# Seven block products for the last wide layer: the second product in three sweeps, with its weight sums made earlier by GpSimd

## The chip, the core and the metric

The kernel runs on one core of a Trainium2 chip. The core has five engines that run their own instruction streams: TensorE (PE in the profile; PEld is its weight load), VectorE (DVE), ScalarE (ACT), GpSimd (POOL) and SyncE (SP, which here only issues DMAs). The metric is device time in microseconds, the median of three runs; lower is better.

## What is computed

A two-layer encoder over 512 tokens of width 1024. Layer 0 has a grouped-query attention and a latent attention side by side, layer 1 a neighbourhood attention with 16 heads. Behind each attention stands a squared-ReLU MLP of width 4096, and at the end an RMS norm. The change touches the MLP of layer 1, and what runs beside the second attention:

```python
def sq_relu_mlp(h, w_up, w_down):
    u = jax.nn.relu(h @ w_up)
    return (u * u) @ w_down
...
        h = h + sq_relu_mlp(rmsnorm(h, norm_ffn[layer]), ffn_w_up[layer], ffn_w_down[layer])
    return rmsnorm(h, final_norm)
```

Everything is float32.

## The kernel before

**Precision.** TensorE works on rounded numbers (fp32r). Each operand is kept as a high part and a low part (`whi`, `wlo` for weights: ACT rounds, DVE subtracts), and a product is three matmuls: high by high, high by low, low by high. The residual stream is kept transposed in SBUF (`hT`, features on the partitions, 8 tiles of 128x512).

**Memory.** 30 slots of 128x1024 float32 are handed out and given back by hand, first in, first out (`Slot`, L65). Raw weights go into a free slot while more than `reserve[0]` are free, otherwise into one of four `raw` buffers. PSUM's eight banks carry four names: mm (3), s (2), t (2), o (1); `group` (L406) hands out four at a time, in turns (`flip`).

**The order of the work.** `plan` (L233) lists the weight groups in the order of their use; `weights(i)` (L237) issues loads five groups ahead of group i and makes high and low parts two groups ahead. A scheduler orders each engine's instructions by when they become ready, except inside `fixed_order` (L957): there TensorE, ACT, DVE and GpSimd run in the order in which the code is written. The second attention runs so. SP's queue is always ordered by the scheduler; every engine takes its own queue strictly in order.

**Plain and seven-product matrix products.** `product` (L415) is the plain one, 512 columns of tokens to a matmul. `Seven` (L314) computes a product of two by two blocks with seven block products instead of eight: the weight blocks are first combined into seven (`seven_chunk`, L295: three GpSimd sums L302 to L304, then ACT L308 and DVE L309), the tokens too (`sums`, `split`), and `Seven.run` (L376) issues 21 matmuls of 256 columns for each pair of tiles (L388 to L390) and combines the seven results when they leave PSUM (L396 to L400).

**The MLP of layer 1** (`mlp`, L1250, called at L1670 with the tail `last`). The 4096 hidden features are 32 tiles of 128. `first_product` (L1110) makes them: six by plain products, the other 26 by thirteen calls of `Seven.run`, two tiles each. `SIZES[1]` = (6, 8, 6, 8, 4) cuts them into stages:

- six tiles (plain), then their part of the second product (plain, 48 groups of three matmuls);
- eight tiles (four calls of `Seven.run`), then their part (plain, 64 groups, L501 to L503);
- six, eight and four tiles (nine calls); the plain part of the six (48 groups), and beside it the DVE makes and splits the token sums of the eight (`convert`, L1243);
- the eight tiles in seven products, four calls of `Seven.run`; beside the last two, `turn(j, 0)` (L1614) transposes the first half of `hT` back to tokens;
- the last four tiles (`down`, L1621), with tokens on the output partitions, mixed with `turn(j, 1)`, the final norm and the stores.

**The second attention** (`attend_C`, L1412). 16 heads, two halves each. In each half TensorE makes the scores of two units, DVE adds the bias (L1441, loaded from DRAM by SP, L1504), ACT takes the exponential (L1460), DVE the reciprocal (L1429), and GpSimd scales (`norm`, L1430). TensorE transposes the result in the next head (`turn`, L1446) and multiplies by the values (`finish`, L1465). `rest` (L1482) calls `norm` twice, and fills TensorE's time in between with work of `fill`: the next projections and the output projection. GpSimd also issues copies of keys and queries (L1338, L1358, L1359); SP issues L1334 and L1363, which follow those.

Of the kernel before, what the change touches and what calls it, by code (L numbers as in the profile page):

```python
# [35 lines left out]
def encoder_kernel(ctx: ExitStack, tc: tile.TileContext, ins, out, dbg=None):  # L36
# [242 lines left out]
    def catch_up():  # L279
        take_up(off_d)  # L280
        take_up(off_a)
# [491 lines left out]
    rope_q(0)  # L773


    kst = Slot()

    def ev_kr(b):
# [331 lines left out]
    def first_product(l):  # L1110
# [7 lines left out]
        xp = [s_.pair() for s_ in X]  # L1118
        U, R = [], []
        rb = keep([P, S], F32, "rb")  # L1120
        state = dict(c=SIZES[l][0], ids=None, plain=False, split=iter(()))
        x7 = Seven(KD)

        def ev(j, b):
# [62 lines left out]
        def ahead():  # L1187
            state["ids"] = x7.plan(w, P * state["c"])

        def stage(n, raw=0, more=0):  # L1190

            if not state["plain"]:
                plain()
            left = n + raw + more - len(U)
            while left:
                i = state["ids"]
                state["c"] += 2
                left -= 2
                if left:
                    ahead()  # L1200
                for _ in x7.run(i, raw_evac if more <= left < more + raw else pair_evac):
# [13 lines left out]
    def bias_rows():  # L1215
        R, Fi, Fe = Slot(F32), Slot(F32), Slot(F32)
        rpb = ins["od_rpb"][0]
        for qr in range(8):
            SP.dma_start(R.t[16 * qr : 16 * qr + 16, 0:248],
                           rpb.rearrange("h a b -> h (a b)")[:, (7 - qr) * 31 : (7 - qr) * 31 + 248])  # L1220
            yield
        POOL.memset(Fi.t[:, 0:376], NEG)
        POOL.memset(Fe.t[:, 256:512], NEG)
        rv = R.t[:, 0:248].rearrange("p (k d) -> p d k", d=31)
        POOL.tensor_copy(Fi.t[:, 0:376].rearrange("p (j k) -> p j k", k=8)[:, 15:31, :], rv[:, 7:23, :])
        POOL.tensor_copy(Fe.t[:, 0:248].rearrange("p (j k) -> p j k", k=8), rv)
# [12 lines left out]
        for s_ in (R, Fi, Fe):  # L1239
            s_.free()  # L1240
        yield

    def convert(u7, R):  # L1243
        held = tc.keep_in_program_order
# [167 lines left out]
    def attend_C(step):  # L1412
# [138 lines left out]
    def step(n):  # L1551
# [3 lines left out]
        if n == 12:  # L1555
# [3 lines left out]
            for x in rest:  # L1559
                fill.add(*x)  # L1560

    fill.run(LEAD)
    with fixed_order():
        fixed[0] = 1
        attend_C(step)
        give_low(len(ready))
        fixed[0] = 0
    ok = [s_.pair() for s_ in O[5:]]
# [8 lines left out]
    def last_mlp():  # L1577
# [43 lines left out]
        def down(k0, c, up, tail):  # L1621
# [33 lines left out]
        def last(k0, tiles_):  # L1655
# [13 lines left out]

        mlp(1, last)  # L1670
        for run in runs:
            run()
        for s_ in V:
# [55 lines left out]
```

## Time and profile before

| | us |
|---|---|
| median of 3 runs | 1183.32 |
| lowest and highest run | 1182.38, 1185.65 |
| span of the profiled execution | 1184.0 |
| second attention | 637 to 816 |
| MLP of layer 1 with the final norm | from 816 |

The profile is of one execution, times are microseconds from its start. Its span is the only time of that execution that is shown, and it lies among the runs. A row of a group of instructions has the line in the kernel, the engine, the operation, what it writes and reads with shapes, the count, then the busy time and the mean duration of one in ns, and last the idle time before them and what ended it. A row in order of time has the start, the length and the engine's instruction, with its idle time and what released it in brackets. Matmuls overlap in TensorE's pipeline, so the time of one is read from the distance between starts, or from a stage's length divided by its count. The granted TensorE clock is 0.994 of full speed over the span.

### The profile page before, as it was taken

The page shows a single profiled execution, that of the slowest core. Times are in us where ns is not written, and L with a number is a line of the kernel's source. Part 1 is how long each engine was busy: PE and PEld are TensorE (multiplying, and loading weights), DVE is VectorE, ACT ScalarE, POOL GpSimd, SP SyncE. Part 2 cuts the span into 40 slices and gives each one's busy share as a digit, 9 for nine tenths or more (in the row PEclk, how much of TensorE's full clock was granted, in tenths as well). Part 3 has the DMA queues.
Part 4 walks back from the last instruction along what each step waited for, and adds up shares of the span by engine and source line. Part 5 has one row for each costly group of instructions (what it writes and reads, how often), then busy time and mean ns, then how long its engine had stood idle before and what let it go on. Part 6 is the DMA issues. An engine that isn't in the chain of part 4 may idle for free.

```text
span 1184.0 us, 19784 instructions
## 1 busy us (share of the span) xinstructions
PE 1160.5 (98%) x7128; PEld 1021.2 (86%) x7128; DVE 883.2 (75%) x1514; ACT 640.3 (54%) x1081; POOL 526.1 (44%) x662
## 2 busy tenths in 40 slices
PE   9989999999999999999999999999999999999997
PEld 8667778888899899988998998988889989998895
DVE  5788998878967368786884676667996736778975
ACT  4468676664546247562553565555554624666344
POOL 3267343224562377819602232231376625774710
PEclk9999999999999999999999999999999999999998
DMA  7223225212524723225226464433352341322412
GB/s 244 71 54 92 68 78 134 62 56 77 167 86 134 263 70 90 72 90 165 67 72 178 131 184 126 116 112 109 107 165 76 115 134 55 98 64 89 143 36 71
DMA packets 110145, 128.01 MB, mean 108 GB/s; under 512 B 9075, under 2 KB 86816, under 8 KB 110048
## 3 DMA queue, kind: packets, MB, share of 16 engines
q1 hardware_dynamic: 106992, 119.30, 33.5%
q0 software_dynamic: 2304, 6.31, 2.2%
q8 instruction: 56, 0.92, 0.3%
q10 hardware_dynamic: 752, 1.15, 0.3%
q14 instruction: 41, 0.34, 0.1%
HBM read 104.32 MB, written 6.29 MB: 93 GB/s over the span
## 4 chain that ended last, share of the span: by engine, by line
PE 81%; DVE 4%; ACT 1%; issue 1%; POOL 0%; DVEq 0%; ACTq 0%
PE mm L503 8%; PE mm L501 8%; PE mm L502 8%; PE mm L390 4%; PE mm L389 4%; PE mm L388 4%; PE t L388 3%; PE t L389 3%; PE t L390 3%; PE s L502 2%; PE s L503 2%; PE s L501 2%; PE s L390 2%; PE s L388 2%; PE s L389 2%; PE s L997 2%
## 5 line engine op out<-in xcount | busy, mean ns | idle before, releaser
L309 DVE TENSOR_TENSOR wlo<-a,whi 128x896 fp32r<-128x896 f32 x132 | 161.8, 1230 | 83.7 <-ACT whi L308 82.9
L308 ACT ACTIVATE whi<-a 128x896 fp32r<-128x896 f32 x132 | 125.0, 950 | 155.0 <-PE o L502 45.8
L501 PE MATMUL mm<-a,whi 128*128 128x512 f32 x485 | 195.9, 406 | 0.9 <-DVE a L915 0.7
L503 PE MATMUL mm<-a,wlo 128*128 128x512 f32 x485 | 192.1, 397 | 2.5 <-DVE wlo L202 2.5
L502 PE MATMUL mm<-a,whi 128*128 128x512 f32 x485 | 192.5, 397 | 0.1
L202 DVE TENSOR_TENSOR wlo<-raw,whi 128x1024 fp32r<-128x1024 f32 (+4 forms) x117 | 139.3, 1193 | 66.4 <-ACT whi L212 63.9
L212 ACT ACTIVATE whi<-raw 128x1024 fp32r<-128x1024 f32 (+3 forms) x120 | 116.4, 971 | 92.2 <-PE s L502 39.8
L302 POOL TENSOR_TENSOR a<-a 128x128 f32<-128x128 f32 x132 | 85.1, 645 | 173.3 <-DMA a<-in_ffn_w_up_dram 103.9
L303 POOL TENSOR_TENSOR a<-a 128x256 f32<-128x256 f32 x132 | 120.2, 910 | 10.3
L304 POOL TENSOR_TENSOR a<-a 128x128 f32<-128x128 f32 x132 | 115.1, 872 | 10.3
L503 PEld LDWEIGHTS mm<-a,wlo 128*128 128x128 f32 x485 | 91.7, 189 | 23.7 <-DVE wlo L202 3.4
L501 PEld LDWEIGHTS mm<-a,whi 128*128 128x128 f32 x485 | 91.8, 189 | 20.4 <-PE t L972 0.9
L502 PEld LDWEIGHTS mm<-a,whi 128*128 128x128 f32 x485 | 91.9, 190 | 17.4 <-DVE a L545 0.4
L388 PE MATMUL mm<-a,whi 128*128 128x256 f32 x370 | 103.9, 281 | 0.0
L389 PE MATMUL mm<-a,whi 128*128 128x256 f32 x370 | 103.9, 281 | 0.0
L390 PE MATMUL mm<-a,wlo 128*128 128x256 f32 x370 | 103.7, 280 | 0.0
L1005 POOL TENSOR_SCALAR p<-p,ti 128x512 f32<-128x512 f32 x64 | 46.2, 724 | 92.3 <-DVE ti L1004 81.1
L1430 POOL TENSOR_SCALAR p<-p,ti 128x256 f32<-128x256 f32 x64 | 35.6, 567 | 104.8 <-DVE ti L1429 91.8
L388 PE MATMUL t<-a,whi 128*128 128x256 f32 x264 | 74.2, 281 | 0.0
L389 PE MATMUL t<-a,whi 128*128 128x256 f32 x264 | 74.1, 281 | 0.0
L390 PE MATMUL t<-a,wlo 128*128 128x256 f32 x264 | 73.9, 280 | 0.0
L390 PEld LDWEIGHTS mm<-a,wlo 128*128 128x128 f32 x370 | 69.6, 188 | 0.2 <-DVE wlo L309 0.2
(338 smaller groups left out, 3210.8 us busy)
## 6 DMA issues: line engine op xcount, KB each, us to landing
a<-in_ffn_w_up_dram SPq DMA_DIRECT2D x104, 256.0 KB
raw<-in_ffn_w_down_dram SPq DMA_DIRECT2D x46, 512.0 KB
raw<-in_od_w_qkv_dram SPq DMA_DIRECT2D x64, 128.0 KB
a<-in_ffn_w_down_dram SPq DMA_DIRECT2D x28, 256.0 KB
raw<-in_ffn_w_up_dram SPq DMA_DIRECT2D x12, 512.0 KB
raw<-in_ev_w_in_dram SPq DMA_DIRECT2D x12, 384.0 KB
a<-a SPq DMA_DIRECT2D x18, 256.0 KB
bias<-bx SPq DMA_DIRECT2D x16, 256.0 KB
```

The lines of the kernel that those rows point to most:

```text
L202: z = lambda: (eng or DVE).tensor_tensor(to, src, f32(high), op=ALU.subtract)
L212: ACT.activation(hi[:, 0:m], raw[:, 0:m], AF.Copy)
L303: POOL.tensor_tensor(r[:, 4:6], r[:, 2:3].to_broadcast([P, 2, P]), r[:, 0:7:6], op=ALU.add)
L304: POOL.tensor_tensor(r[:, 7], r[:, 3], r[:, 5], op=ALU.subtract)
L308: ACT.activation(hi[:, 0:896], raw[:, 128:1024], AF.Copy)
L309: DVE.tensor_tensor(lo[:, 0:896], raw[:, 128:1024], f32(hi[:, 0:896]), op=ALU.subtract)
L388: PE.matmul(o, wh, x[:, 0], start=kp == 0 and n in (0, 1, 3, 5), stop=False, skip_group_check=True)
L389: PE.matmul(o, wh, x[:, 1], start=False, stop=False, skip_group_check=True)
L390: PE.matmul(o, wl, x[:, 0], start=False, stop=kp == self.np - 1, skip_group_check=True)
L501: PE.matmul(o, wh, xh, start=first, stop=False)
L502: PE.matmul(o, wh, xl, start=False, stop=False)
L503: PE.matmul(o, wl, xh, start=False, stop=last)
```

## The change

Layer 1's MLP becomes `mlp_swept`. Its first six tiles are done as before. Then all other 26 tiles of the first product are made one after the other, in thirteen calls of `Seven.run`: 22 stay raw (high and low parts are not made yet), the last four go to `down` as before. The 22 raw tiles are 11 pairs, and their part of the second product is one product of two by two blocks (pair by output half by token half), with the sums of seven products kept in six PSUM banks X, Y and Z over all pairs. It runs as three sweeps over the pairs (two, two and three block products to a pair); `tokens` makes what tokens a step needs, GpSimd the sums among them. The weight sums that sweeps 1 and 2 need are made by `SumsAhead` during the second attention: two loads of 512 KB and four GpSimd sums of 128x512 to a pair, each stored to DRAM (`made`) by SP; one step of it follows each `norm` until the 44 are done. `turn(j, 0)` moves behind the first tiles of `down`. Layer 0 keeps `mlp`.

The diff, cut; left out are the definitions that follow directly from it (`line`, `blocks`, the body of `stage`, the last part of `mlp_swept`):

```diff
+    FIRST, RAW, MORE = 6, (26, 22), (0, 4)
...
+    class SumsAhead:
...
+        def load(self, kp):
+            if kp < self.n:
+                self.raw[kp] = Slot(F32), Slot(F32)
+                for z, s_ in enumerate(self.raw[kp]):
+                    k = self.k0 + 2 * kp + z
+                    SP.dma_start(s_.t, self.w[k * P : (k + 1) * P, :])
+
+        def steps(self):
+            self.load(0)
+            yield
+            for kp in range(self.n):
+                self.load(kp + 1)
+                two = self.raw.pop(kp)
+                (a11, a21), (a12, a22) = ((blocks(s_.t)[:, 0], blocks(s_.t)[:, 1]) for s_ in two)
+                to = self.made[kp]
+                POOL.tensor_tensor(a22, a21, a22, op=ALU.add)
+                SP.dma_start(line(to[0, :, S:]), a22)
+                yield
+                POOL.tensor_tensor(a21, a11, a21, op=ALU.subtract)
+                SP.dma_start(line(to[1, :, 0:S]), a21)
+                yield
+                POOL.tensor_tensor(a11, a22, a11, op=ALU.subtract)
+                SP.dma_start(line(to[0, :, 0:S]), a11)
+                yield
+                POOL.tensor_tensor(a12, a12, a11, op=ALU.subtract)
+                SP.dma_start(line(to[1, :, S:]), a12)
+                for s_ in two:
+                    s_.free()
+                yield
...
+    def sweep_chunk(w, k0, kind, made):
...
+        sa, a = raw()
+        sb, b = raw() if kind == 2 else (None, None)
+        if kind == 0:
+            for z in range(2):
+                SP.dma_start(line(a[:, S * z : S * z + S]), half(k0 + z, 0))
+        else:
+            SP.dma_start(a, made[kind - 1])
+        if kind == 2:
+            SP.dma_start(line(b[:, 0:S]), half(k0 + 1, 1))
+        yield
...
+        ACT.activation(hi, a, AF.Copy)
+        DVE.tensor_tensor(lo, a, f32(hi), op=ALU.subtract)
+        third = None
+        if kind == 2:
+            third = Slot()
+            ACT.activation(third.t[:, 0:S], b[:, 0:S], AF.Copy)
+            DVE.tensor_tensor(third.t[:, S:], b[:, 0:S], f32(third.t[:, 0:S]), op=ALU.subtract)
...
+    class Sweeps:
...
+        def tokens(self, kind, kp):
...
+            if kind == 0:
+                split_to(d[:, :, 0], d[:, :, 1], r[:, 0:4:2])
+                POOL.tensor_tensor(r[:, 0:2], r[:, 1:4:2], r[:, 0:2], op=ALU.subtract)
+                POOL.tensor_tensor(s2, r[:, 3], r[:, 0], op=ALU.subtract)
+            elif kind == 1:
+                for q, src in enumerate((r[:, 0], s2)):
+                    split_to(d[:, q, 0], d[:, q, 1], src)
+                POOL.tensor_tensor(r[:, 2], s2, r[:, 2], op=ALU.subtract)
...
+            else:
+                split_to(d[:, :, 0], d[:, :, 1], r[:, 1:3])
...
+        def run(self, R):
...
+            PRODUCTS = [
+                [(X, 0, at(0)), (Z, 1, at(S))],
+                [(Y, 0, at(S)), (X, 1, at(0))],
+                [(Y, 2, at(S)), (Z, 1, lambda h, m: (h[2].t[:, 0:S], h[2].t[:, S:], P * m)), (X, 0, at(0))],
+            ]
+
+            def mm(kind, n, m, w_, x, first, last):
...
+                PE.matmul(o, wh, x[:, 0], start=first and m % 2 == 0, stop=False, skip_group_check=True)
+                PE.matmul(o, wh, x[:, 1], start=False, stop=False, skip_group_check=True)
+                PE.matmul(o, wl, x[:, 0], start=False, stop=last, skip_group_check=True)
...
+            for i, (kind, kp) in enumerate(steps):
+                if i + 1 < len(steps):
+                    ready_[steps[i + 1]] = self.tokens(*steps[i + 1])
+                w_ = weights(self.ids[kind][kp])[0]
...
+                lead = (0, 0, 1)[kind]
+                todo = [(kp, w_, x, lead)] + waiting
+                waiting = []
+                others = [(kp, w_, x, n) for n in range(len(PRODUCTS[kind])) if n != lead]
+                if kp == 0 and kind:
+                    waiting = others
+                else:
+                    todo += others
...
+    def mlp_swept(l, made, last=None):
...
+        reserve[0] = 3
+        sweeps = []
+        R, V = stage(0, RAW[l], MORE[l], lambda: sweeps.append(Sweeps(w, FIRST, made)))[1:]
+        reserve[0] = 6
...
             for x in w:
                 norm(*x)
+                next(sums1, None)
...
+    ahead1 = SumsAhead(ins["ffn_w_down"][1], FIRST, RAW[1] // 2)
+    sums1 = ahead1.steps()
+    next(sums1)
...
+                if c == 0:
+                    for j in range(4):
+                        turn(j, 0)
...
-            def beside(m, i):
-                if m == 2 and i == 0:
+            def beside(kind, kp):
+                if (kind, kp) == (2, 6) and not H:
...
-                if m > 1 and i in (16, 22):
-                    turn(2 * (m - 2) + (i == 22), 0)
...
-        mlp(1, last)
+        mlp_swept(1, ahead1, last)
+        flip[0] = 1
```

More of the change, by code (lines that the diff above doesn't have):

```diff
@@ L773, in encoder_kernel, with line, blocks, __init__ @@
     rope_q(0)
+    FIRST, RAW, MORE = 6, (26, 22), (0, 4)
+    def line(t):
+        return t.rearrange("p (z n) -> p z n", z=2)
+    def blocks(t):
+        return t.rearrange("p (z f n) -> p f z n", z=2, f=2)
+    class SumsAhead:
+        def __init__(self, w, k0, n):
+            self.w, self.k0, self.n = w, k0, n
+            self.made = dr.tile([n, 2, P, 1024], F32, name=nm("made"))
+            self.raw = {}
+        def load(self, kp):
[26 more added lines that the diff above has]
+                yield
     kst = Slot()
@@ L1188, in ahead, with stage @@
             state["ids"] = x7.plan(w, P * state["c"])
-        def stage(n, raw=0, more=0):
+        def stage(n, raw=0, more=0, then=lambda: None):
             if not state["plain"]:
@@ L1241, in bias_rows, with raw, half @@
         yield
+    def sweep_chunk(w, k0, kind, made):
+        def raw():
+            slot = Slot(F32) if len(free) > reserve[0] else None
+            return slot, slot.t if slot else wp.tile([P, 1024], F32, tag="raw", bufs=4, name=nm("raw"))
+        def half(k, f):
+            return w[k * P : (k + 1) * P, :].rearrange("p (z f n) -> p f z n", z=2, f=2)[:, f]
+        sa, a = raw()
[8 more added lines that the diff above has]
+        yield
+        hi = wp.tile([P, 1024], F32R, tag="whi", name=nm("whi"))
+        lo = wp.tile([P, 1024], F32R, tag="wlo", name=nm("wlo"))
+        ACT.activation(hi, a, AF.Copy)
[5 more added lines that the diff above has]
+            DVE.tensor_tensor(third.t[:, S:], b[:, 0:S], f32(third.t[:, 0:S]), op=ALU.subtract)
+        for s_ in (sa, sb):
+            if s_:
+                s_.free()
+        yield (hi, lo, third), None, []
@@ new lines, in mlp_swept, with ev @@
+    def mlp_swept(l, made, last=None):
+        stage, ahead, later = first_product(l)
+        w = ins["ffn_w_down"][l]
+        bias = bias_rows() if l == 0 else iter(())
+        U = stage(FIRST)[0]
+        up = [s_.pair() for s_ in U]
+        def ev(m, b):
+            DVE.tensor_tensor(hT[:, m, :], hT[:, m, :], b, op=ALU.add)
+        gens = [product(w, 0, up, tiles(512 * c, 512), lambda j, b, c=c: ev(4 * c + j, b)) for c in range(2)]
+        ahead()
+        for c, gen in enumerate(gens):
+            for i, _ in enumerate(gen):
+                later(c, i)
+        for s_ in U:
+            s_.free()
+        reserve[0] = 3
+        sweeps = []
+        R, V = stage(0, RAW[l], MORE[l], lambda: sweeps.append(Sweeps(w, FIRST, made)))[1:]
+        reserve[0] = 6
+        beside = last(FIRST + RAW[l], V) if last else lambda kind, kp: next(bias, None)
+        for kind, kp in sweeps[0].run(R):
+            beside(kind, kp)
+        for _ in bias:
+            pass
+        reserve[0] = 1
@@ L1565, in encoder_kernel @@
         attend_C(step)
+        assert next(sums1, 0) == 0 and not ahead1.raw
         give_low(len(ready))
```

86 lines of the change are left out of this document (85 added, 1 removed).

## The prediction

> **What bounds the kernel now.** I read the page first (busy time and the chain that ended last), then a table by stage of the last layer, then the matmuls of one line in the same stages.
>
> ```profile
> span 1184.0 us, 19784 instructions
> ...
> PE 1160.5 (98%) x7128; PEld 1021.2 (86%) x7128; DVE 883.2 (75%) x1514; ACT 640.3 (54%) x1081; POOL 526.1 (44%) x662
> ...
> PE 81%; DVE 4%; ACT 1%; issue 1%; POOL 0%; DVEq 0%; ACTq 0%
> ```
>
> TensorE is busy 98% of the span and carries 81% of the chain: work taken from TensorE shortens the kernel as long as the other engines still deliver. The span of this execution, 1184.0 us, lies inside the three runs (1182.38 to 1185.65); nothing else around it is shown. I sum against 1184.0 and take off 0.7 at the end, since the median is 1183.32.
>
> The next view is the busy time by stage: start and end, length, then busy time and instruction count of PE, PEld, DVE, ACT and POOL, granted clock, DMA share, GB/s. The stages are: the second attention; the first product's four runs behind eight wide tiles; the plain second product over those eight; nine more runs of the first product; the plain second product over six tiles; the second product in seven products over eight tiles.
>
> ```profile
> 637.00:816.00 179.00, 178.36 (x1103) 157.76 (x1102) 120.22 (x329) 99.20 (x237) 50.51 (x92) 1.00 0.50 139
> 898.46:938.14 39.68, 39.68 (x337) 39.68 (x336) 29.16 (x33) 25.40 (x32) 23.91 (x31) 1.00 0.23 67
> 938.14:982.64 44.50, 44.50 (x194) 36.06 (x193) 20.64 (x24) 11.41 (x13) 15.46 (x21) 1.00 0.41 131
> 982.64:1071.96 89.32, 89.32 (x757) 89.32 (x756) 68.22 (x76) 57.94 (x73) 60.40 (x75) 1.00 0.27 78
> 1071.96:1109.36 37.40, 35.17 (x146) 28.20 (x145) 33.86 (x48) 15.48 (x23) 23.38 (x27) 0.95 0.36 111
> 1109.36:1150.86 41.50, 41.50 (x353) 41.49 (x352) 32.23 (x36) 18.89 (x24) 15.51 (x20) 1.00 0.24 77
> ```
>
> Five of the six have TensorE busy throughout. Between 1071.96 and 1109.36 it is not: DVE is busy 33.86 of 37.40 us, since there it also makes the token-side sums (convert, L1243). TensorE's rows there show one long wait:
>
> ```profile
> 1102.58 0.79 PE L503 MATMUL mm<-a,wlo 128*128 128x512 f32 x1 [2.23 <-DVE wlo L202]
> ```
>
> **The change part by part.** First the matmuls. The same stages, counting only the first of each three matmuls (L501 at 512 columns, L388 at 256):
>
> ```profile
> 938.14:982.64 44.50, 25.25 (x64) 11.91 (x64) 1.00 0.41 131
> 1071.96:1109.36 37.40, 19.51 (x48) 9.34 (x48) 0.95 0.36 111
> ```
>
> ```profile
> 898.46:938.14 39.68, 31.39 (x112) 20.86 (x111) 1.00 0.23 67
> 1109.36:1150.86 41.50, 31.78 (x112) 20.84 (x111) 1.00 0.24 77
> ```
>
> *Removed from TensorE.* The plain products over 8 and 6 wide tiles: 3 x 64 = 192 matmuls in 44.50 us (0.232 us each) and 3 x 48 = 144 in 37.40 us (0.260 us each, the stall above included): 81.90 us. The seven-product stage over eight tiles: 336 matmuls of 256 columns and the 16 transposes of turn(j, 0), 41.50 us. Together 123.40 us.
>
> *Added.* Sweeps.run over 11 pairs of tiles: sweep 0 has two block products a pair, sweep 1 two, sweep 2 three; each is four output tiles by three matmuls of 256 columns. 11 x 7 x 12 = 924 matmuls. A 256-column matmul takes 39.68 / 336 = 0.1181 us, so 109.1 us. The 16 transposes move to the last product (down, c == 0); they cost 41.50 - 336 x 0.1181 = 1.8 us in the old place, and I charge the same. Net: 123.4 - 109.1 - 1.8 = 12.5 us less, 1171.5 us if nothing else is late. The first product keeps its thirteen runs, only placed end to end.
>
> *GpSimd's sums in the attention.* SumsAhead.steps puts 44 sums of 128x512 (four a head, heads 0 to 10) between the softmax normalisations (L1430) in GpSimd's hand-written order. GpSimd's rows over the whole kernel give the prices (busy, mean ns):
>
> ```profile
> L303 POOL TENSOR_TENSOR a<-a 128x256 f32<-128x256 f32 x132 | 120.2, 910 | 10.3
> ...
> L1430 POOL TENSOR_SCALAR p<-p,ti 128x256 f32<-128x256 f32 x64 | 35.6, 567 | 104.8 <-DVE ti L1429 91.8 <-PE o L1472 9.7 <-PE mm L1388 3.2
> ...
> L517 POOL TENSOR_TENSOR acc<-acc,sc 128x512 f32<-128x512 f32 x5 | 6.7, 1339 | 19.2 <-ACT sc L515 19.2
> ```
>
> At 1.34 us a sum (L517) this is 59 us on an engine that is busy 50.51 us of 179. Whether it fits is decided by half a head. The chain of waits has the attention's score matmuls 31 half heads apart:
>
> ```profile
> 639.70 0.48 PE s L1426 x4
> ...
> 805.08 0.48 PE s L1426 x4
> ```
>
> (805.08 - 639.70) / 31 = 5.33 us. GpSimd would have two normalisations (1.13 us), two sums (2.68) and its DMA issues: of the stage's 92 POOL instructions 28 are no normalisation, which at what is left of the busy time, (50.51 - 64 x 0.567) / 32, is 0.44 us. That is 4.25 of 5.33: it fits, with 1.1 us spare. Behind a sum stand the next normalisation and the key and query copies that GpSimd issues (L1338, L1358, L1359); for the normalisation waits TensorE's transpose in the next head. In one head the transpose waits for it already:
>
> ```profile
> 745.67 0.33 PE L1452 MATMUL t<-cst,p 128*128 128x128 f32 x1 [0.16 <-POOL p L1430]
> ```
>
> Lower end 0 (every sum fits into GpSimd's gaps; no gain is possible, as nothing leaves the attention). Upper end: the sums also wait for DVE, as the rows below show for a 128x128 sum (1.19 instead of 0.46 us): 1.34 + 0.73 = 2.07 us (and DVE's subtractions in their turn behind the sums) against the (5.33 - 1.13 - 0.44) / 2 = 1.88 us that fit, 44 x 0.19 = 8 us. I take 2.5 us, nearer the lower end, by L517, whose operands have the same shape: half heads with 1.1 us spare, and a transpose that waits already.
>
> *Their DMAs.* SP gets 22 loads of 512 KB and 44 stores of 256 KB more; each store waits for its sum, and behind it on SP's queue stand the bias loads (L1504), the weight loads (L190, L193) and the copies L1334 and L1363. The bias of head 4 (fifth of 16) is issued at
>
> ```profile
> 665.29 0.37 SPq L1504 DMA_DIRECT2D bias<-bx x1
> ```
>
> and first needed when head 4 has its scores, eight half heads in, 639.70 + 8 x 5.33 = 682.3, some 17 us later; a store that waits one half head (5.33 us) uses a third of it. I charge nothing; with that cover gone DVE would wait for the bias once a head. The 23.1 MB are the larger question, kept for the rivals.
>
> *The first product's runs end to end.* GpSimd's sums (L302 to L304) are close to TensorE's pace there. In one part of the nine runs GpSimd was busy 41.41 of 44.08 us with 51 sums, three to a group of weights: 2.59 us a group, while TensorE used 21 x 0.1181 = 2.48 a group:
>
> ```profile
> 1015.47:1059.55 44.08, 44.08 (x375) 44.08 (x374) 34.01 (x39) 28.57 (x34) 41.41 (x51) 1.00 0.29 86
> ```
>
> Four more runs are 16 more groups, 16 x 0.11 = 1.8 us of lead lost. TensorE did not wait in the nine runs (89.32 us for 756 matmuls is 0.1181 each). 0 to 1.8, I take 0.5: raw tiles spare DVE the splits that made it slow GpSimd.
>
> *Sweep 0.* A step gives TensorE 24 x 0.1181 = 2.83 us. DVE subtracts once over 128x1024 and once over 128x512; GpSimd makes a 128x512 and a 128x256 sum (Sweeps.tokens). DVE's prices in the attention, and how the two engines meet in the first product's runs:
>
> ```profile
> L202 DVE TENSOR_TENSOR wlo<-raw,whi 128x1024 fp32r<-128x1024 f32 x18 | 22.0, 1223 | 0.2 <-ACT whi L212 0.2
> ...
> L830 DVE TENSOR_TENSOR a<-sc,a 128x512 fp32r<-128x512 f32 x14 | 9.9, 710 | 5.7 <-ACT a L833 5.7
> ```
>
> ```profile
> 1003.79 1.55 DVE L309 TENSOR_TENSOR wlo<-a,whi 128x896 fp32r<-128x896 f32 x1
> ...
> 1019.66 1.09 DVE L309 TENSOR_TENSOR wlo<-a,whi 128x896 fp32r<-128x896 f32 x1 [1.96 <-ACT whi L308]
> ```
>
> ```profile
> 1004.48 1.19 POOL L304 TENSOR_TENSOR a<-a 128x128 f32<-128x128 f32 x1
> ...
> 1019.34 0.46 POOL L304 TENSOR_TENSOR a<-a 128x128 f32<-128x128 f32 x1
> ```
>
> The same subtraction takes 1.09 us once and 1.55 beside GpSimd; the same sum 0.46 and 1.19 beside DVE. They take turns. Laid end to end, a step is 1.22 + 0.71 + 1.34 + 0.91 = 4.18 us, 1.35 over TensorE's, 11 x 1.35 = 14.9 us in all, less the two groups of weights that are ready ahead (2 x 2.83): 9.2 us. The lower end is 0: in the 44.08 us above, the two also shared the time and TensorE lost none; GpSimd bore it. Here GpSimd may fall behind even further, its sums being read eleven steps later. I take 1.5 us. The Trainium skill, "SBUF — State Buffer", section "Who interferes with whom", says that a VectorE instruction with two SBUF inputs and a GpSimd instruction that reads SBUF exclude each other for the whole instruction. By it the end-to-end figure would be right; the trace shows the turns, though looser: the 1.19 us at 1004.48 fall within DVE's 1.55 from 1003.79 for 0.86 us.
>
> *Small ones, together.* Where sweep 1 and sweep 2 begin, DVE must empty two and four banks, which the matmuls fill again 24 matmuls (2.83 us) later. At L830's 0.71 us for 128x512, behind one subtraction of 1.22, that is 2.6 and 4.1 us: 0 to 1.3, I take 1.0. The four turns in a row share two banks, so the third waits for a copy of 128x512: 0.7, priced by the same row. DVE's token sums of 1071.96 to 1109.36 are gone, and their stall is in the removed 37.40.
>
> Sum: 1184.0 - 12.5 + 2.5 + 0.5 + 1.5 + 1.0 + 0.7 = 1177.7; minus 0.7 for the median: 1177.0 us.
>
> **The rivals.**
> *Everything is covered.* The charges all vanish: 1171.5 - 0.7 = 1170.8. For it: TensorE lost next to nothing to such overlaps up to now; against it: the transpose above waits already.
>
> *DVE and GpSimd take strict turns in sweep 0.* 9.2 us in place of 1.5: 1184.7, no change. For it: the 1.55 and 1.19 rows; against it: the 44.08 us without loss. It decides once DVE's two subtractions and their waits exceed 2.83 us a step. The rule of the Trainium skill above ("SBUF — State Buffer", "Who interferes with whom") is for it.
>
> *The DMA engines pace the attention (slower).* Heads 0 to 10, and a stretch of the first MLP with dense traffic, by the last two columns (DMA share and GB/s):
>
> ```profile
> 639.50:757.00 117.50, 117.34 (x771) 106.41 (x770) 77.94 (x222) 67.21 (x159) 35.40 (x68) 1.00 0.55 148
> 405.00:415.00 10.00, 10.00 (x45) 8.10 (x44) 2.33 (x2) 0.99 (x2) 5.63 (x9) 1.00 0.98 343
> ```
>
> The change adds 23.1 MB, 196 GB/s over 117.5 us; at 343 GB/s for 0.98 that is 0.56 more share, 1.11 in all. Then the loads come 0.11 x 117.5 = 12.9 us late over the stage, GpSimd stands at the sum whose load is missing, the normalisations behind it are late and TensorE stands at the transposes: 1177.0 - 2.5 + 12.9 = 1187.4, slower. It decides from a share of 1 on. Against it: 0.55 counts time that packets waited on each other in bursts, and a load asked for a head (10.7 us) ahead absorbs most of such a lag.
>
> **How the numbers follow.** Forecast 0.50, all covered 0.17, strict turns 0.14, DMA-paced 0.15, something else 0.04. A measurement of this kernel tells about 0.3% (3.5 us) from no change. Faster (below 1179.8): 0.48 + 0.17 + 0.03 = 0.68. Same: 0.02 + 0.09 + 0.05 + 0.01 = 0.17. Slower (above 1186.9): 0.02 + 0.10 + 0.03 = 0.15. The range runs from the covered case, 1170.5, to just short of the DMA-paced one, 1187: it takes in the attention's 8 us and sweep 0's 9.2 us one at a time.
>
> **What would show it.** Right: 924 matmuls at 0.118 us in one stretch of about 111 us; no PE row in the sweeps with a wait above 1 us except where a sweep begins; attention within 3 us of 179; GpSimd's new sums at 1.3 to 1.8 us. Wrong: PE waiting for DVE's wlo in sweep 0 over 5 us in total (strict turns); GpSimd waiting for DMA at the new sums and a DMA share near 1 with half heads longer than 5.6 us (DMA-paced); matmuls of 256 columns slower than 0.12 us.

## The result, and the profile after

The changed kernel takes 1201.98 us (median of four runs, 1200.58 to 1203.1), the kernel before 1183.11 in the same comparison: a ratio of 1.0152, 95% interval 1.0136 to 1.0168. The forecast of 1177.0 was 25 us too low, it said faster where the kernel became slower, and its range ended at 1187. From the page of the changed kernel, the span, the busy times and the engines' shares of the chain:

```profile
span 1201.3 us, 20600 instructions
...
PE 1159.6 (97%) x7380; PEld 1032.5 (86%) x7380; DVE 899.1 (75%) x1521; ACT 657.6 (55%) x1116; POOL 588.2 (49%) x691
...
PE 77%; DVE 6%; DMA 2%; issue 1%; ACT 1%; POOL 1%; DVEq 0%; ACTq 0%; POOLq 0%; SPq 0%
```

TensorE's busy time hardly fell (1160.5 before), the span grew by 17.3 us, and the DMA engines stand in the chain with 2%, where they were not listed before. The busy times by stage, in the columns of the prediction's table: the second attention, its heads 0 to 10, the thirteen runs of the first product, and sweeps 0, 1 and 2:

```profile
637.00:832.00 195.00, 183.51 (x1100) 161.33 (x1099) 123.41 (x329) 99.72 (x236) 107.63 (x136) 0.97 0.76 227
639.00:757.00 118.00, 110.35 (x674) 97.63 (x672) 72.27 (x194) 60.25 (x142) 79.86 (x96) 0.97 0.93 278
914.42:1043.52 129.10, 129.10 (x1093) 129.10 (x1092) 97.36 (x109) 81.15 (x99) 100.65 (x121) 1.00 0.32 92
1043.52:1082.53 39.01, 33.01 (x267) 31.77 (x265) 36.79 (x33) 20.14 (x32) 31.85 (x24) 1.00 0.57 192
1082.53:1119.08 36.55, 33.24 (x266) 32.83 (x265) 30.50 (x41) 21.23 (x36) 9.49 (x8) 0.95 0.65 202
1119.08:1166.04 46.96, 46.96 (x399) 46.96 (x398) 29.82 (x41) 20.91 (x30) 0.00 (x0) 1.00 0.30 107
```

The time came from two places. From the first to the last score matmul the second attention takes 182.4 us (639.02 to 821.39), before 165.7: 16.6 us more. The sweeps take 39.01 + 36.55 + 46.96 = 122.52 us for 924 matmuls, where 109.1 would do: 13.4 us lost, all in sweeps 0 and 1 (sweep 2: 396 x 0.1181 = 46.8). So the stages that replace 123.40 us are 0.9 shorter and not 14 shorter. The tail behind the sweeps grew from 33.14 to 35.26 us with the sixteen transposes of `turn(j, 0)` that moved there. 16.6 - 0.9 + 2.1 is 17.8; 0.5 less lies ahead of the first score, which leaves the 17.3.

**In the attention** GpSimd's sums cost what was forecast, and none of them waits for its load (the last column is the idle time before the group):

```profile
L809 POOL TENSOR_TENSOR a<-a 128x512 f32<-128x512 f32 x11 | 14.6, 1330 | 0.0
L806 POOL TENSOR_TENSOR a<-a,a 128x512 f32<-128x512 f32 x11 | 14.2, 1291 | 0.0
```

What waits can be followed in the chain of waits that ends in TensorE's longest stop there, 3.85 us at 760.33 (some pieces are left out), and in the rows of GpSimd and of SP ahead of it:

```profile
749.02 5.12 DMA made<-a
754.24 0.64 ACT a L878
754.90 0.69 DVE a L875
755.59 0.33 DVE p L1680
...
759.39 0.90 POOL p L1669
760.33 0.47 PE t L1691
```

```profile
743.02 1.29 POOL L812 TENSOR_TENSOR a<-a,a 128x512 f32<-128x512 f32 x1
```

```profile
748.45 0.47 SPq L1573 DMA_DIRECT2D a<-a  x1
749.02 0.53 SPq L813 DMA_DIRECT2D made<-a  x1
```

The store at 749.02 (L813) belongs to the sum L812, which had ended at 744.31. For 4.7 us the store could not be issued, as SP's queue stood ahead of it: SP was busy with weight loads until 745.04, and then the copy L1573 waited for a key copy of GpSimd's to land. Then the store took 5.12 us to land, and only then may ACT (L878) write into the slot that the store read, 9.8 us after the sum's end. DVE's subtraction stands behind ACT, the next bias additions behind that in DVE's queue, then GpSimd's normalisation, then TensorE's transpose. Earlier in that chain a weight load stands with 3.31 us (at 725.11).

**In the sweeps** TensorE waits for one thing (us in total, times, longest):

```profile
PE t L1389 <- DVE wlo L1312: 6.0, 6, 3.7
PE mm L1389 <- DVE wlo L1312: 3.3, 2, 2.4
```

The groups of DVE and of GpSimd, 1043.52 to 1091, in two views:

```profile
L1312 DVE TENSOR_TENSOR wlo<-a,whi 128x1024 fp32r<-128x1024 f32 x9 | 15.1, 1690 | 0.0
L1341 DVE TENSOR_TENSOR a<-a,a 128x512 fp32r<-128x512 f32 x9 | 9.8, 1111 | 0.7 <-ACT a L1340 0.7
```

```profile
L1346 POOL TENSOR_TENSOR a<-a 128x512 f32<-128x512 f32 x9 | 15.0, 1669 | 8.8 <-ACT a L1340 4.8 <-DVE a L1341 4.0
L1347 POOL TENSOR_TENSOR a<-a 128x256 f32<-128x256 f32 x11 | 14.2, 1300 | 0.3
L1351 POOL TENSOR_TENSOR a<-a,a 128x256 f32<-128x256 f32 x10 | 11.9, 1201 | 0.2
```

These waits add up to 9.3 of the 13.4 us. Part of the rest is the clock: between 1087.95 and 1091.30, behind the longest wait of sweep 1, the granted clock was 0.50, and the matmuls start 0.21 us apart in place of 0.12, which costs some 1.7 us. DVE's subtraction of 128x1024 takes 1.69 us on average (1.22 in the prediction's row), and GpSimd makes all three sums of a pair here: the scheduler has pulled L1351, a sum for sweep 1, into sweep 0.

### The profile page after: what moved, and what is told of

It is laid out like the page before. It is cut to its first block, busy times and chain, and to the rows that moved or that the text cites. A ratio compares the mean times of both kernels' runs of the same rounds, so it can differ in the third digit from the quotient of the medians.

```text
span 1201.3 us, 20600 instructions
## 1 busy us (share of the span) xinstructions
PE 1159.6 (97%) x7380; PEld 1032.5 (86%) x7380; DVE 899.1 (75%) x1521; ACT 657.6 (55%) x1116; POOL 588.2 (49%) x691
## 4 chain that ended last, share of the span: by engine, by line
PE 77%; DVE 6%; DMA 2%; issue 1%; ACT 1%; POOL 1%; DVEq 0%; ACTq 0%; POOLq 0%; SPq 0%
PE mm L501 6%; PE mm L503 6%; PE mm L502 6%; PE mm L390 3%; PE mm L389 3%; PE mm L388 3%; PE t L389 2%; PE t L388 2%; PE t L390 2%; PE s L502 2%; PE s L503 2%; PE s L501 2%; PE s L390 2%; PE s L388 2%; PE s L389 2%; PE s L1042 2%
## 5 line engine op out<-in xcount | busy, mean ns | idle before, releaser
L309 DVE TENSOR_TENSOR wlo<-a,whi 128x896 fp32r<-128x896 f32 x116 | 143.3, 1239 | 68.0 <-ACT whi L308 67.5
L501 PE MATMUL mm<-a,whi 128*128 128x512 f32 x443 | 179.6, 407 | 0.9 <-DVE a L960 0.7
L308 ACT ACTIVATE whi<-a 128x896 fp32r<-128x896 f32 x116 | 109.8, 949 | 127.8 <-PE o L502 36.6
L503 PE MATMUL mm<-a,wlo 128*128 128x512 f32 x443 | 175.4, 397 | 2.3 <-DVE wlo L202 2.3
L502 PE MATMUL mm<-a,whi 128*128 128x512 f32 x443 | 176.0, 397 | 0.1
L202 DVE TENSOR_TENSOR wlo<-raw,whi 128x1024 fp32r<-128x1024 f32 (+4 forms) x103 | 124.4, 1211 | 48.7 <-ACT whi L212 48.5
L302 POOL TENSOR_TENSOR a<-a 128x128 f32<-128x128 f32 x116 | 77.0, 664 | 97.2 <-DMA a<-in_ffn_w_up_dram 67.3
L503 PEld LDWEIGHTS mm<-a,wlo 128*128 128x128 f32 x443 | 83.9, 190 | 21.6 <-DVE wlo L202 3.1
L304 POOL TENSOR_TENSOR a<-a 128x128 f32<-128x128 f32 x116 | 97.6, 842 | 9.1
L501 PEld LDWEIGHTS mm<-a,whi 128*128 128x128 f32 x443 | 83.8, 189 | 18.4 <-PE t L1017 0.9
L502 PEld LDWEIGHTS mm<-a,whi 128*128 128x128 f32 x443 | 84.2, 190 | 15.6 <-DVE a L545 0.4
L389 PE MATMUL mm<-a,whi 128*128 128x256 f32 x330 | 92.7, 281 | 0.0
L388 PE MATMUL mm<-a,whi 128*128 128x256 f32 x330 | 92.5, 280 | 0.0
L389 PE MATMUL t<-a,whi 128*128 128x256 f32 x232 | 65.2, 281 | 0.0
L388 PE MATMUL t<-a,whi 128*128 128x256 f32 x232 | 65.0, 280 | 0.0
L390 PEld LDWEIGHTS mm<-a,wlo 128*128 128x128 f32 x330 | 62.1, 188 | 0.2 <-DVE wlo L309 0.2
```

The lines of the kernel that those rows point to most:

```text
L202: z = lambda: (eng or DVE).tensor_tensor(to, src, f32(high), op=ALU.subtract)
L304: POOL.tensor_tensor(r[:, 7], r[:, 3], r[:, 5], op=ALU.subtract)
L308: ACT.activation(hi[:, 0:896], raw[:, 128:1024], AF.Copy)
L309: DVE.tensor_tensor(lo[:, 0:896], raw[:, 128:1024], f32(hi[:, 0:896]), op=ALU.subtract)
L388: PE.matmul(o, wh, x[:, 0], start=kp == 0 and n in (0, 1, 3, 5), stop=False, skip_group_check=True)
L389: PE.matmul(o, wh, x[:, 1], start=False, stop=False, skip_group_check=True)
```

## The experiments

The theories: *D*, the added transfers lengthen the attention; *G*, GpSimd's added sums do; *T*, DVE and GpSimd slow each other in the sweeps. First, each suspect was taken away. Where no interval is given, a kernel ran once; how well a span repeats can be seen from e4, whose attention is that of the change: 182.5 us there, 182.4 in the change.

**e1_no_sums_ahead.** No loads, sums or stores in the attention.

```diff
-            self.load(0)
-            for kp in range(self.n):
+            for kp in range(0):
...
-            SP.dma_start(a, made[kind - 1])
+            SP.dma_start(a, w[(k0 + kind - 1) * P : (k0 + kind) * P, :])
```

> Left out: everything that the change puts into the second attention (the 22 loads, 44 sums and 44 stores); sweeps 1 and 2 load plain rows of the weight, of the same size, in place of the stored sums. Both theories of the attention (D: the added transfers come near what the DMA engines can carry and make biases, slots and weights late; G: GpSimd's added sums hold up the softmax normalisations) expect its first and last score matmul 165 to 167 us apart again, against 182.0 with the change, and a time of 1184 to 1187 us. Theory T (in the sweeps DVE and GpSimd slow each other) expects the sweeps to keep their 120 to 123 us. The rival for the sweeps, that their own loads suffer from what the attention leaves behind in the DMA queues, expects them 5 us shorter or more.

1185.31 us (before 1183.8 on the same chip); attention 165.8, sweeps 121.1. The attention is whole again, and the sweeps' loss is their own: 121.1 - 109.1 = 12.0 us, nearly the 12.5 that the change should bring.

**e2_dma_only**, **e3_sums_only** and **e5_no_stores** leave one part of the work in the attention, or two.

```diff
# e2, all four sums alike
+                POOL.tensor_tensor(a22[:, :, 0:4], a21[:, :, 0:4], a22[:, :, 0:4], op=ALU.add)
# e3
+                two = self.raw[0]
# e3 and e5, all four stores alike
-                SP.dma_start(line(to[0, :, S:]), a22)
```

> Changed: each of the 44 sums covers 4 columns of each half only, all loads and stores stay. D (DMA) expects the attention's score matmuls to stay 180 to 183 us apart and a time of 1199 to 1203 us. G (GpSimd's sums) expects 165 to 168 us apart and 1184 to 1188 us. Sweeps 120 to 123 us by both.

> Changed: the 44 sums of full size all work on one pair of weight rows that is loaded once; no other added load and no store; sweeps 1 and 2 load plain rows of the weight in place of the stored sums. D (DMA) expects the attention's score matmuls 165 to 168 us apart and a time of 1184 to 1188 us; G (GpSimd's sums) expects 180 to 183 us and 1199 to 1203 us. Sweeps 120 to 123 us by both.

> Left out: the 44 stores of the sums in the second attention (loads and sums of full size stay; sweeps 1 and 2 load plain rows of the weight). Theory S (the time goes where a tile may be used again only when its store has landed) expects the attention's score matmuls within 1.5 us of the 167.2 us without any added DMA. Theory D (the total traffic, whose half is left) expects 170 to 176 us. Sweeps 120 to 123 us by both.

e2 took 1191.81 us, e3 1187.02 (before 1183.8); e5 1186.85 (before 1184.71). The first to the last score matmul, with all the runs on the attention that follow below:

| in heads 0 to 10, unless said otherwise | us | over before |
|---|---|---|
| nothing (e1) | 165.8 | 0.1 |
| sums alone (e3) | 167.2 | 1.5 |
| loads and sums (e5) | 167.1 | 1.4 |
| loads, sums, stores of 4 columns (e6) | 172.0 | 6.2 |
| loads and stores, sums of 4 columns (e2) | 172.7 | 6.9 |
| all, stores issued later (h1) | 176.1 | 10.4 |
| all, tiles of their own (i1) | 180.2 | 14.4 |
| all (the change) | 182.4 | 16.6 |
| all, stores on GpSimd's queue (g1) | 191.3 | 25.6 |
| all, over 16 heads (g2) | 172.1 | 6.4 |
| five pairs over 16 heads (f1) | 165.9 | 0.2 |

Neither D nor G holds alone: transfers without the sums cost 6.9, sums without the transfers 1.5, both 16.6. Beside the sums the loads are harmless, as S of e5 has it, and the stores are not. The DMA issues in 639 to 757 show what they do to others. These copies go through GpSimd's queue, so no store stands ahead of them on SP's (KB, then the median time to landing): before, with loads and sums only, and with the change.

```profile
a<-a POOLq DMA_DIRECT2D x12, 256.0 KB, 3.4
```

```profile
a<-a POOLq DMA_DIRECT2D x12, 256.0 KB, 3.7
```

```profile
a<-a POOLq DMA_DIRECT2D x10, 256.0 KB, 5.4
```

**e4_no_token_sums.** The sweeps without GpSimd.

```diff
-                POOL.tensor_tensor(r[:, 0:2], r[:, 1:4:2], r[:, 0:2], op=ALU.subtract)
-                POOL.tensor_tensor(s2, r[:, 3], r[:, 0], op=ALU.subtract)
-                for q, src in enumerate((r[:, 0], s2)):
+                for q, src in enumerate((r[:, 0], r[:, 3])):
-                POOL.tensor_tensor(r[:, 2], s2, r[:, 2], op=ALU.subtract)
```

> Left out: the sums of token operands that GpSimd makes in sweeps 0 and 1 (the splits read the tiles as they are). T (DVE and GpSimd slow each other in sweep 0) expects the sweeps at 109 to 113 us in place of 122.5, no wait of TensorE there above 1 us, DVE's 128x1024 subtraction back near 1.2 us, and a time of 1188 to 1193 us. Rival 1 (the sweeps' loads are late, DMA share 0.70 in sweep 0) and rival 2 (emptying the banks at the start of sweeps 1 and 2) expect 119 us or more for the sweeps and 1198 us or more. The attention stays at 180 to 183 us.

The sweeps take 111.35 us as T expects, with steps of 2.83 us, and yet the kernel takes 1200.33 us: ahead of the first sweep TensorE now stands for 10.25 us. The chain there:

```profile
1046.56 0.61 DVE a L400
...
1047.25 1.07 ACT a L1193
1048.34 1.06 ACT a L1194
1049.42 0.64 ACT a L878
1050.09 1.30 DVE a L875 x2
1051.41 0.64 ACT a L1339
```

Without the sums the scheduler placed the split of the very first step (L1339) behind the last run's evacuation (L400 to L1194) on ACT. So the total says nothing for or against T; the runs with a mended order below do.

**f1_spread, f2d_spread_dve, f2p_spread_pool.** Six pairs are made in the first attention, five over all heads of the second; in f2d and f2p the token sums besides are two of 128x256 a step in sweeps 0 and 1, on DVE or on GpSimd.

```diff
+        if n >= 38:
+            next(sums0, None)
...
+                turn_[0] += 1
+                if turn_[0] % 3 == 0:
+                    next(sums1, None)
# f2d; f2p has POOL in place of DVE
+                held(DVE.tensor_tensor(r[:, 0], r[:, 1], r[:, 0], op=ALU.subtract))
+                held(DVE.tensor_tensor(s2, r[:, 3], r[:, 0], op=ALU.subtract))
...
+                held(DVE.tensor_tensor(r[:, 1], r[:, 3], r[:, 1], op=ALU.subtract))
+                held(DVE.tensor_tensor(r[:, 2], s2, r[:, 2], op=ALU.subtract))
```

> Changed only in when the sums are made: six of the eleven pairs in the second half of the first attention (one sum after each of its steps from the 39th on), five over all 16 heads of the second attention (one sum after every third normalisation). Theory DG (the second attention loses time where added traffic and added GpSimd work meet in heads 0 to 10; each alone cost 6.8 and 1.4 us, both 16.6) expects the second attention's score matmuls 165 to 169 us apart, the first attention at most 3 us longer, and a time of 1184 to 1189 us. Rival (each sum with its load and stores costs TensorE the same wherever it is made) expects 8 us or more lost in the first attention and a time of 1195 us or more.

> As the spread version, and the token sums of the sweeps are made by DVE instead of GpSimd, two of 128x256 a step in sweeps 0 and 1. DVE then has 1.21 + 0.69 + 2 x 0.41 = 2.72 us a step against TensorE's 2.83. Theory T (DVE and GpSimd slow each other in sweep 0) expects the sweeps at 110 to 115 us in place of 122.5 and a time of 1173 to 1179 us. Rival (DVE is the bound by itself, with the banks to empty and a late start) expects 118 us or more and a time above 1181 us.

> As the spread version, and GpSimd's token sums are balanced: two of 128x256 a step in sweeps 0 and 1, in that order, none of sweep 1 ahead. If DVE and GpSimd exclude each other for whole instructions, a step needs 1.21 + 0.69 + 2 x 0.73 = 3.36 us against TensorE's 2.83: the sweeps take 115 to 121 us, the time is 1178 to 1186 us. If they mostly overlap, the sweeps take 110 to 114 us and the time is 1173 to 1179 us.

| | us | ratio to before, 95% | first attention, scores | second | sweeps |
|---|---|---|---|---|---|
| before | 1184.71 | | 171.7 | 165.7 | |
| f1 | 1195.1 | 1.0066 to 1.0116 | 180.2 | 165.9 | 122.7 |
| f2d | 1182.71 | 0.9974 to 0.9998 | 179.6 | 165.9 | 110.2 |
| f2p | 1188.11 | 1.0018 to 1.0044 | 178.4 | 165.9 | 115.8 |

The second attention bears five pairs for 0.2 us. The first attention loses 6.7 to 8.5 us to the other six, so f1's expectation was missed, and the times of f2d and f2p lie above theirs. The rival's numbers came out in f1, but its reason, the same cost wherever a sum is made, does not fit the 0.2. In the first attention GpSimd does wait for a load, as in the prediction's third rival. Its group in 160 to 255 of f1:

```profile
L807 POOL TENSOR_TENSOR a<-a,a 128x512 f32<-128x512 f32 x6 | 8.6, 1431 | 12.7 <-DMA a<-in_ffn_w_down_dram 9.7 <-PE t L1022 3.0
```

Nearly all of the 9.7 is one wait that ends at 216.65. TensorE does not stop at it: its stops next to it are 0.68 us at 200.80 and 0.40 at 226.56. In the whole stretch TensorE stops 5.2 us for the normalisation and 2.8 for DVE; what makes these late is not shown.

T holds. Of the 12.5 us between f1's sweeps and f2d's, 6.9 come already in f2p, where GpSimd makes sums of the same size in all, but spread evenly over sweeps 0 and 1 and in a fixed order; the last 5.6 come from the engine alone, although DVE is the busier one. DVE's rows at the start of the sweeps, in f2d and in f2p:

```profile
L1320 DVE TENSOR_TENSOR wlo<-a,whi 128x1024 fp32r<-128x1024 f32 x12 | 14.5, 1216 | 0.0
...
L1350 DVE TENSOR_TENSOR a<-a,a 128x256 fp32r<-128x256 f32 x14 | 5.3, 415 | 0.0
...
L1355 DVE TENSOR_TENSOR a<-a 128x256 f32<-128x256 f32 x9 | 3.7, 416 | 0.0
```

```profile
L1320 DVE TENSOR_TENSOR wlo<-a,whi 128x1024 fp32r<-128x1024 f32 x11 | 17.3, 1583 | 0.4 <-ACT whi L1319 0.4
L1350 DVE TENSOR_TENSOR a<-a,a 128x256 fp32r<-128x256 f32 x15 | 12.1, 852 | 1.6 <-ACT a L1349 1.6
```

Beside GpSimd DVE's 0.42 us become 0.85. In f2p a step needs 3.36 us if the engines take turns (the expectation's sum): 22 steps of 0.53 more than TensorE's, less two steps of lead (5.7), are 6.0 us; measured 115.8 - 110.2 = 5.6. The nearness is partly luck: TensorE's waits in f2p's sweeps are 3.3 us, and some 1.7 come from a granted clock of 0.50 between 1069.20 and 1072.60. The rule of the Trainium skill ("SBUF — State Buffer", "Who interferes with whom") that a VectorE instruction with two SBUF inputs and a GpSimd instruction that reads SBUF exclude each other for the whole instruction agrees with DVE's 0.42 becoming 0.85; the size of the loss bears it out only as far as those 3.3 us of waits.

**g1_stores_on_pool, g2_sixteen_heads, g3_pool_sixteen_dve.** Whether the stores hurt by standing on SP's queue (Q) or by their bytes (L).

```diff
# g1, g3: all four stores
-                SP.dma_start(line(to[0, :, S:]), a22)
+                POOL.dma_start(line(to[0, :, S:]), a22)
# g2, g3
-                next(sums1, None)
+                norms[0] += 1
+                if 44 * norms[0] // 64 > 44 * (norms[0] - 1) // 64:
+                    next(sums1, None)
```

> Changed: the 44 stores of the sums are issued from GpSimd's own queue, behind the sum that they store, and no longer from SP's; bytes, sums and their places stay. Theory Q (the stores wait on SP's queue for GpSimd's sums, and the weight, bias and slot traffic behind them on that queue comes late) expects the second attention's score matmuls 166 to 172 us apart in place of 182.4 and a time of 1185 to 1192 us. Theory L (the traffic itself, 23.1 MB more, and slots that wait for a store to land) expects 178 us or more and 1197 us or more.

> Changed: the 44 sums are spread evenly over the 64 normalisations of all 16 heads of the second attention, in place of one at each of the first 44; the stores stay on SP's queue. The traffic per head falls to 11/16, by the DMA share of the kernel before to 0.55 + 0.39 = 0.94. L (traffic) expects the score matmuls 167 to 175 us apart and 1186 to 1195 us. Q (SP's queue) expects most of the loss to stay, 176 us or more and 1195 us or more, since every store still waits for its sum on that queue.

> Three changes at once: stores on GpSimd's queue, sums spread over all 16 heads, and the sweeps' token sums on DVE (two of 128x256 a step in sweeps 0 and 1). The sweeps should stay at 110 to 111 us, as in the run with DVE's sums. By Q, and by Q and L together, the second attention's score matmuls are 165.5 to 169 us apart and the time is 1171 to 1176 us; if neither change helps the attention, 180 us and 1186 us or more.

g1 took 1211.11 us and g2 1198.17 (before 1183.79); g3 1179.9, ratio 0.995 to 0.9977, with 168.3 us of attention and 110.1 of sweeps; its time lies above the 1171 to 1176 that were expected. g2 is as L expects in the attention; its total lies above L's range, since the sums now run into the last head: from the last score to the first product 96.7 us pass in place of 93.0, with a wait of 1.63 us at 823.08. g1 says nothing on Q, because it makes G true: issuing a store costs GpSimd 0.77 us.

```profile
L807 POOL DMA_DIRECT2D made<-a x11 | 8.4, 768 | 3.3 <-POOL a L806 3.3
```

The 44 issues are 34 us more on an engine that had 1.1 us a half head to spare: 16.6 of TensorE's 17.0 us of waits in that attention are for its normalisation. Over 16 heads it has the room: in the second attention g3 and g2 differ only in the queue of the stores, and the 168.3 us against 172.1 give that queue 3.8 of g2's 6.4 us.

**e6_small_stores, h1_stores_later, h2_later_sixteen_dve.**

```diff
# e6, all four stores
+                SP.dma_start(line(to[0, :, S:])[:, :, 0:4], a22[:, :, 0:4])
# h1, h2: a store is kept back and issued two sums later
+                    if len(late) == 2:
+                        late.pop(0)()
...
+                    late.append(lambda o=o, dst=dst, then=done if i == 3 else lambda: None:
+                                (SP.dma_start(line(dst), o), then()))
```

> Changed: each of the 44 stores carries only 4 columns of each half (its place on SP's queue, its wait for the sum and the tile's release after it stay; the loads and the sums keep their size; sweeps 1 and 2 load plain rows of the weight). Theory Q (SP's queue stands at a store until GpSimd has made its sum, and what is queued behind comes late) expects the second attention's score matmuls 177 to 183 us apart, as with full stores. Theory L (the stores' bytes: traffic, and tiles that are released only when a store of 256 KB has landed) expects 167 to 170 us, as without the stores (167.1).

> Changed: each store is issued on SP two sums later than its sum, so that SP need not wait for GpSimd; a pair's tiles are released that much later, and the next pair is loaded one sum later. All bytes and sums stay in heads 0 to 10. Q expects the score matmuls 167 to 172 us apart and 1186 to 1191 us. L expects 179 us or more and 1198 us or more.

> Three changes at once: the later stores (still on SP), the sums spread over all 16 heads, and the sweeps' token sums on DVE. The sweeps stay at 110 to 111 us. By Q the attention's score matmuls are 165.5 to 168 us apart and the time is 1176 to 1180 us; by L they stay at 170 to 173 us, as with the spreading alone (172.1), and the time is 1181 to 1186 us.

e6 took 1194.47 us and h1 1193.9 (before 1184.26). Both fall between Q and L: without the bytes 4.8 us above the sums alone stay, and 10.4 of the 16.6 go; issuing later takes 6.3 away. h1 is also no clean test, for SP still stood 29.9 us at its stores, by its own waits. In e6 a store of 4 columns, issued as soon as its sum was there, takes as long to land as the full one above:

```profile
739.26 1.29 POOL a L815
740.56 5.32 DMA made<-a
745.90 0.64 ACT a L878
```

h2 takes 1176.76 us with 166.9 us of attention, ratio 0.9934, interval 0.9917 to 0.9951: the fastest here. Against g2, at the same rate, the later stores (and loads one sum later) save 5.2 of the 6.4 us. Its heads 0 to 10, and its sweeps:

```profile
640.00:757.00 117.00, 116.05 (x756) 104.80 (x756) 81.24 (x217) 67.00 (x158) 74.50 (x97) 1.00 0.88 258
```

```profile
1030.33:1140.53 110.20, 109.88 (x927) 109.67 (x926) 92.73 (x154) 62.95 (x96) 0.00 (x0) 1.00 0.53 180
```

**i1_own_tiles, i2_own_sixteen_dve.** In e6 and in the changed kernel the longest waits led to a slot that had been handed on under a store (theory R). In h1 DVE stood 14.7 us in two waits for a bias instead.

```diff
+            self.own = [(Slot(F32), Slot(F32)) for _ in range(3)]
...
+                two = self.own[kp % 3]
...
+                self.load(kp + 2)
```

> Changed: the sums keep six tiles of their own through the attention (three pairs in turn, a pair loaded two sums into the pair before the last one's end) and give none back to the common list; sums, stores, bytes, queue and heads 0 to 10 stay. Theory R (the common list hands a tile on while the store out of it has not landed, and the conversion that gets it waits 4 to 6 us, with the normalisations behind it) expects the second attention's score matmuls 167 to 171 us apart in place of 182.4 and a time of 1186 to 1191 us. Rival (SP's queue standing at the stores, or the bytes themselves) expects 176 us or more and 1195 us or more.

> Three changes at once: four tiles of the sums' own (two pairs in turn), the sums spread over all 16 heads, and the sweeps' token sums on DVE. R expects 166 to 168 us between the attention's first and last score matmul, 110 to 111 us of sweeps and 1174 to 1178 us. Rival (with only two pairs a load stands on SP's queue until the stores out of its tiles have landed, and what is behind it is late) expects 170 us or more and 1179 us or more.

R falls in heads 0 to 10: i1 took 1199.4 us (before 1183.8). No conversion waits for a store any more; now a load of the next pair does (L795), on SP's queue, and DVE stands 12.2 us for a bias that SP issues at 709.04, 3.6 us after DVE was ready for it, and that lands 8.6 us later. From i1's waits of DVE, and of SP:

```profile
DVE p L1682 <- DMA bias<-bx: 12.8, 2, 12.2
```

```profile
SPq L795 <- DMA made<-a: 12.9, 7, 3.8
```

i2 took 1179.53 us (0.995 to 0.9977) with 168.8 us of attention: between R and its rival, 3.3 less than g2. So the victim changes with the arrangement, and at the full rate most of the lateness stays. What is shown is that the stores make it, that their bytes (e6) and their place on SP's queue (g3 against g2) both have a part, and that it shrinks with the rate: 16.6 us over 11 heads, 6.4 over 16, 0.2 with five pairs over 16. At the rate of 16 heads another queue, a later issue or tiles of their own each win back 3.3 to 5.2 of the 6.4. How the 15 us of the change divide between bytes, queue and held tiles stays open: what their removal wins one by one (10.4, 6.3 and 2.2) adds up to more than the 15.

## Why the prediction was wrong, point by point

- **The matmuls: right.** 129.10 us for the thirteen runs (0.118 each, nothing lost, 0.5 charged: the prediction's 2.59 us a group is the stage's length and counts GpSimd's idle time, where its busy 41.41 us are 2.44 a group, less than TensorE's 2.48), and 110.2 us for the 924 where no engine holds them up (109.1 forecast). The transposes cost 2.1 us of 2.5 charged.
- **GpSimd's sums in the attention: right.** 1.28 to 1.33 us each (1.34 forecast); alone they cost 1.5 us (2.5 taken).
- **Their DMAs: "I charge nothing" failed.** With the transfers the attention loses 16.6 us. The prediction worked out the cover of the bias alone, and that mostly held: DVE waits for a bias once, 3.2 us. But weights, copies and handed-on slots share SP's queue and the DMA engines with 44 stores, and each store holds a tile until it has landed; for that nothing was charged. The third rival had the sign and nearly the size (12.9) but the wrong path: it had GpSimd stand at a missing load, and in the changed kernel no sum waits for one. The reason against it, that loads are asked for a head ahead, is true of the loads (1.4 us with all of them) and says nothing of stores; the other reason, its reading of the share of 0.55, is borne out by no run.
- **Sweep 0: "I take 1.5 us" failed; with the starts of sweeps 2.5 was charged, and 13.4 was lost.** The strict turns were the better model: TensorE's waits for DVE's `wlo` are 9.3 us, their sum was 9.2. That these agree so well is luck, as the sum left out L1351, the sum for sweep 1 (1.2 us here), which ran in sweep 0, and the slower clock. The row that made 1.5 look safe, GpSimd 41 of 44 us busy without loss to TensorE, came from a stage with one DVE subtraction a step; here there are two.
- **Both at once.** Each failure had a rival of its own, and none combined them; 0.68 for faster needed both to stay small. They are 14.1 and 10.9 us over what was charged, and the other terms give 1.4 back: 23.6 between the sum of 1177.7 and the span of 1201.3. With both mended the gain is there: h2 takes 1176.76 us against 1184.26, 7.5 less, where 6.3 were forecast. It is another kernel, so it is chance that its time lies next to 1177.0.

## What to carry to other kernels

Work that is hidden on an idle engine brings its stores along: price each store by the tile that it holds until it lands, by what stands ahead of it on its queue and by what is behind it. The DMA share alone is no price: in 639 to 757 it is 0.81 in e6 (6.2 us lost), 0.88 in h2 (1.2), 0.97 in e2 (6.9) and 0.93 in the change (16.6). Two engines that slow each other are to be summed over everything that the scheduler may pull into the stretch; one engine doing both jobs can be faster. Where two rivals are independent, price them together.

## What was not expected of the hardware

Around the waits in the attention TensorE is also granted less clock: 0.50 in 726.10 to 729.50, 732.95 to 736.30 and 760.30 to 763.60. The stretch 720 to 740 of the changed kernel:

```profile
720.00:740.00 20.00, 16.16 (x72) 13.33 (x71) 13.29 (x34) 11.43 (x25) 12.44 (x15) 0.83 0.86 287
```

About 1 us behind the wait at 725.10, 512-column matmuls start 0.43 us apart for some 2.5 us, where they start 0.23 apart ahead of it: TensorE's waits of over 0.25 us add up to 11.2 of the 16.6, and part of the rest is this. Before the change no such stretch falls into the second attention. And a store of 4 columns, in as many pieces as the full one (two to a partition), took as long to land (5.32 us) as one of 256 KB (5.12): in these two cases its own bytes did not set when it landed.
